# Convolution weights, conditioning columns and the copied sums outside the stages' pools, discarded products in PSUM, one unit moved, in a two-layer transformer step

## The chip, the cores and the metric

One NeuronCore of a Trainium2 chip runs one program. The metric is device microseconds of that core for one execution; a version's time is the median of its runs. Engines in the text: TensorE (PE), VectorE (DVE), ScalarE (ACT), GpSimd (POOL) and SyncE (SP, which here only issues DMAs).

## The reference

Two sequences of 128 tokens (a prompt and a sample with cached context of 128 more) pass through two layers with 2048 features, in fp32. Each layer has six modulation vectors of 2048 entries per sequence: shift, scale and gate for the mixer (j = 0, 1, 2) and for the feed-forward part (j = 3, 4, 5). Layer 0's mixer joins latent attention and grouped-query attention, layer 1's is differential attention. All weights come from memory once.

```
mod = silu(cond) @ w_ada[l] + b_ada[l]          # 2048 -> 6 * 2048, for each sequence
h = rmsnorm(x, g_norm_mix[l]) * (1 + sc1) + sh1
x = x + gt1 * mixer(h)
h = rmsnorm(x, g_norm_ffn[l]) * (1 + sc2) + sh2
u = h @ w_up                                    # 2048 -> 2 * 5632
u = u[t-1] * w_conv[0] + u[t] * w_conv[1] + u[t+1] * w_conv[2] + b_conv
x = x + gt2 * ((silu(gate) * val) @ w_down)     # gate, val: the halves of u
```

## The kernel before

Both sequences are kept side by side: a tile of activations has 128 features on the partitions and 2 x 128 tokens along it. A product (`gemm`, L226) takes blocks of 128x128 weights; each weight and each activation is split in a high and a low part (`split`, L186: ACT casts, DVE subtracts), and three matmuls per block (L233 to L235) add up in one PSUM tile, `acc`, of which there are three. A weight tile of 1 MB (`raw`, three buffers) is loaded by SyncE (L208) and split into `wh` and `wl` of 8 blocks each, four buffers of each (L215, L216). An up product has 16 blocks (48 matmuls), a down product 22 (66).

The program runs in stages: `ab` (layer 0's mixer: input projection, heads, output projection), `ffn0`, `c` (layer 1's mixer), `ffn1`. Each stage opens its own pool of SBUF tiles, which lies over the memory of the pools closed before it; what is needed throughout lies in the pool `keep`. All eight PSUM banks are given out once: `pacc` 3, `pada` 1, `patt` 3, `pmisc` 1 (L83 to L86).

**The modulation vectors** are made beside the rest. One unit (l, j, q) is a quarter of one vector, 512 entries, from 4 MB of `w_ada` in four loads. There are three ways:

- A unit in the list `ROWS` is normally summed on PE (`sum_rows`, L318): the weights move, the conditioning columns (`condw`, 32 columns per block) stand (L322), into the bank `ada`. ACT copies the sums to SBUF as `am` (L263), PE transposes them (L269), and DVE adds them up and adds the bias `bada` (L278, L280).
- If its index is in `SUMMED`, DVE multiplies and adds the weights (L348, L351) into `aacc`, and PE only sums over the partitions (L256, four matmuls) before the copy and two transposes.
- A unit in the list `FEATS` is made of eight feature steps (L306): DVE multiplies 2048 weights by a row of the conditioning (`condb`) and adds up on the way. The products themselves are thrown away: they are written to `junk`, a bf16 tile in the FFN's pool. L313 adds the bias.

`pump(rows, feats)` (L372) is called after every product and issues as many of these steps as have come due by the stage's rate: `RATE` for rows, `FRATE` for feature steps (0.68 per up product, 1.47 per down product; none in the first three pairs of up products and in the last four down products). `RLIMIT` and `FLIMIT` say up to which unit a stage may go. `fill(units)` issues whole units at once, at the start of `ffn0`, `c` and `ffn1`, while the norm is made and modulated (`modulated`, L433). A scheduler then orders the instructions of each engine by a simulated timeline; calls in `keep_in_program_order` stay in their order.

**Who owns which tile.** `condw` is built by `set_condw` (L117) at the start of `ab` in the pool `rows` and again at the start of `c` in the pool `cc`: POOL clears it, ACT fills two of 32 columns. `am` and `aacc` lie in the same pools. The convolution's weights `convw` (176 KB) lie in the FFN's pool and are loaded at its start (L851, L854). The convolution itself (`conv`, L857) reads `acc`: ACT multiplies and adds the bias (L859), DVE adds the two neighbours (L862, L865). At the start of `ffn` and of `c` a list of tiles is made in advance (L850 to L853, L925 to L928), which lays the pool out in that order.

**Order at an FFN's start.** `modulated` issues `ensure`, the norm, the modulation of 16 chunks and `fill`; then `ffn` loads `convw`, and products run with their convolutions. `load_row` (L292) loads `condb` (2 MB) and applies silu after the first product.

Of the kernel before, what the change touches and what calls it, by code (L numbers as in the profile page):

```python
# [17 lines left out]
P = 128  # L18
# [19 lines left out]
    ("cond", 32), ("bada", NL * 6 * 32),  # L38
    ("gmix", NL * 32), ("gffn", NL * 32), ("gfin", 16),
# [9 lines left out]
RATE = {"in": 0.4, "in3": 0.25, "heads": 0.85, "out0": 1.2, "c": 0.75, "outc": 0.75}  # L49
FRATE = {"up": 0.68, "down": 1.47}  # L50
# [10 lines left out]
ROWS += [(1, 2, 1), (1, 2, 2), (1, 2, 3)]  # L61
# [13 lines left out]
def step_kernel(ctx: ExitStack, tc: tile.TileContext, A: dict):  # L75
# [41 lines left out]
    def set_condw(pl):  # L117
        ada["condw"] = T_(pl, [P, KD, 32], "condw")
        pool.memset(ada["condw"], 0.0)
        act.activation(ada["condw"][:, :, 0:2], C("cond").rearrange("p (k r) -> p k r", r=2), AF.Silu)  # L120
# [34 lines left out]
    def rstd(ps, n):  # L155

        v = T_(small, [P, 16], "rv")
        dve.tensor_scalar(out=v[:, :n], in0=ps, scalar1=EPS, scalar2=None, op0=ALU.add)
        r = T_(small, [P, 16], "rr")
        pool.tensor_tensor(out=r[:, :n], in0=v[:, :n], in1=C("mhalf")[:, :n], op=ALU.pow)  # L160
        return r
# [84 lines left out]

    def ada_finish(l, j, q, on_dve):
# [3 lines left out]
        def reduce():  # L251
            ps = T_(pada, [P, 512], "ada")
# [13 lines left out]
        def turn():  # L266
            pt = T_(pada, [P, 512], "ada")
# [3 lines left out]
            bias = C("bada").rearrange("p (l j k r) -> p l j k r", l=NL, j=6, k=KD)[:, l, j, 4 * q:4 * q + 4]  # L271
# [13 lines left out]
    def scales(l, j, q, out):  # L285
        if j in (1, 4):
            g_ = C("gmix" if j == 1 else "gffn").rearrange("p (l k r) -> p l k r", l=NL, k=KD)
            dve.scalar_tensor_tensor(out=scl[:, l, j // 4, 4 * q:4 * q + 4], in0=out, scalar=1.0,
                                     in1=g_[:, l, 4 * q:4 * q + 4], op0=ALU.add, op1=ALU.mult)
# [8 lines left out]
    def feature_step():  # L298
# [4 lines left out]
        if c == 0:  # L303
# [3 lines left out]
            out=T_(feat["pool"], [P, D], "junk", mybir.dt.bfloat16), in1=feat["row"][:, c],  # L307
# [765 lines left out]
```

## Time and profile before

| | |
|---|---|
| runs before | 2515.49, 2517.92, 2518.29 us; median 2517.92 us |
| profiled execution | 2521.01 us, span 2518.9 us, granted clock 0.983 |
| instructions | 47341 |
| DMA | 613 MB, 243 GB/s over the span |
| stages in the span (about) | `ab` to 484 us, `ffn0` to 1268 us, `c` to 1716 us, `ffn1` to 2507 us |

A page of the profile gives each engine's busy time, then 40 slices of the span with the busy share in tenths, then the chain of work that ended last, then groups of instructions. `L233 PE MATMUL acc<-hx,wh` is the instruction of line 233, which reads `hx` and `wh` and writes `acc`; `x4208 | 1199.8, 286 | 22.1` are its count, its busy time in us, the mean of one in ns, and the idle time of the engine just before these instructions. A view of waits says `PE acc L233 <- DVE cv L865: 14.6, 2, 8.2`: matmuls of line 233 waited 14.6 us in all for line 865 on DVE, two times, at most 8.2 us. A timeline gives start and length in us, and in brackets how long the engine had been idle and what released it. Matmul records overlap: one lasts 0.28 us, but in a stretch without a gap the next starts 0.12 us later.

### The profile page before, as it was taken

How to read it: one execution, taken by the hardware profiler on the slowest of the kernel's cores; microseconds unless marked ns; L12 is line 12 of the kernel's file. 1: busy time of each engine (PE TensorE's matmuls, PEld its weight loads, DVE VectorE, ACT ScalarE, POOL GpSimd, SP SyncE). 2: the span in 40 equal slices, each digit the busy share in tenths (PEclk: the TensorE clock that was granted, in tenths of full speed). 3: DMA queues.
4: the chain of work that ended last, by engine and by line, in shares of the span. 5: the costliest groups of instructions: out<-in, count | busy, mean ns of one | idle time of the engine just before them, and what ended most of it. 6: DMA issues, size and time to landing. Idle time of an engine off the chain costs nothing.

```text
span 2518.9 us, 47341 instructions
## 1 busy us (share of the span) xinstructions
PE 2440.5 (97%) x19674; PEld 2300.5 (91%) x19674; DVE 1775.3 (70%) x2715; ACT 1155.7 (46%) x1817; POOL 173.0 (7%) x212
## 2 busy tenths in 40 slices
PE   6999999989999999999999999998999999999997
PEld 3778868789999999999979999896999999999997
DVE  2457534558888888889869897885787645666644
ACT  3335543454443344544455454435544433555442
POOL 2002101200000000001210100021000000000011
PEclk8999999999999999999999999998999999999999
DMA  9886667766667776667776777677565555555553
GB/s 378 311 306 239 246 247 296 292 251 250 250 232 262 282 268 247 234 252 266 268 278 236 277 247 280 224 300 303 201 251 185 184 182 181 182 182 181 183 183 117
DMA packets 92549, 613.05 MB, mean 243 GB/s; under 512 B 9968, under 2 KB 17840, under 8 KB 20400
## 3 DMA queue, kind: packets, MB, share of 16 engines
q1 hardware_dynamic: 92336, 610.04, 66.5%
q8 instruction: 154, 2.52, 0.4%
q14 instruction: 59, 0.48, 0.1%
HBM read 605.25 MB, written 4.75 MB: 242 GB/s over the span
## 4 chain that ended last, share of the span: by engine, by line
PE 95%; DMA 2%; DVE 1%; issue 1%; ACT 1%; POOL 0%; POOLq 0%; SPq 0%; DVEq 0%; ACTq 0%
PE acc L233 29%; PE acc L234 29%; PE acc L235 29%; PE ada L322 4%; DMA araw<-w_ada 1%; PE att L493 1%; DMA raw<-w_ada 1%; PE ada L269 1%; DMA raw<-w_in_ab 0%; DMA convw<-wconv 0%; PE att L782 0%; PE att L483 0%; PE ada L256 0%; DVE x L941 0%; ACT wh L187 0%
## 5 line engine op out<-in xcount | busy, mean ns | idle before, releaser
L187 ACT CAST wh<-raw 128x1024 fp32r<-128x1024 f32 (+1 forms) x788 | 790.4, 1008 | 1136.9 <-PE acc L234 955.8
L188 DVE TENSOR_TENSOR wl<-raw,wh 128x1024 fp32r<-128x1024 f32 (+1 forms) x788 | 925.6, 1182 | 493.7 <-ACT wh L187 479.5
L233 PE MATMUL acc<-hx,wh 128*128 128x256 f32 x4208 | 1199.8, 286 | 22.1 <-DVE cv L865 14.6
L234 PE MATMUL acc<-hx,wh 128*128 128x256 f32 x4208 | 1198.3, 285 | 0.0
L235 PE MATMUL acc<-hx,wl 128*128 128x256 f32 x4208 | 1196.5, 285 | 0.0
L233 PEld LDWEIGHTS acc<-hx,wh 128*128 128x128 f32 x4208 | 810.3, 193 | 52.8 <-ACT cv L859 14.9
L234 PEld LDWEIGHTS acc<-hx,wh 128*128 128x128 f32 x4208 | 811.3, 193 | 23.6 <-issue 20.0
L235 PEld LDWEIGHTS acc<-hx,wl 128*128 128x128 f32 x4208 | 811.2, 193 | 12.2 <-issue 12.1
L234 PE MATMUL acc<-g,wh 128*128 128x256 f32 x1408 | 398.2, 283 | 0.0
L235 PE MATMUL acc<-g,wl 128*128 128x256 f32 x1408 | 398.0, 283 | 0.0
L233 PE MATMUL acc<-g,wh 128*128 128x256 f32 x1408 | 397.8, 283 | 0.0
L234 PEld LDWEIGHTS acc<-g,wh 128*128 128x128 f32 x1408 | 270.3, 192 | 0.0
L235 PEld LDWEIGHTS acc<-g,wl 128*128 128x128 f32 x1408 | 270.2, 192 | 0.0
L233 PEld LDWEIGHTS acc<-g,wh 128*128 128x128 f32 x1408 | 270.1, 192 | 0.0
L306 DVE CUSTOM_DVE_ANT_0 junk<-araw,condb 128x2048 bf16<-128x2048 f32 x112 | 255.5, 2281 | 0.0
L153 POOL TENSOR_TENSOR sqacc<-sqacc,sq 128x256 f32<-128x256 f32 x76 | 94.2, 1240 | 1650.3 <-issue 1319.7
L322 PE MATMUL ada<-araw,condw 128*32 128x512 f32 x864 | 122.1, 645 | 22.2 <-DMA araw<-w_ada 20.1
L351 DVE SCALAR_TENSOR_TENSOR aacc<-araw,condw,aacc 128x512 f32<-128x512 f32 x180 | 132.7, 763 | 0.3
L859 ACT ACTIVATE cv<-acc,convw 128x256 f32<-128x256 f32 x176 | 98.2, 560 | 10.2 <-DMA convw<-wconv 10.2
L444 DVE SCALAR_TENSOR_TENSOR x<-acc,mod,x 128x128 f32<-128x128 f32 x192 | 58.1, 344 | 61.4 <-PE acc L235 61.4
L862 DVE SCALAR_TENSOR_TENSOR cv<-acc,convw,cv 128x254 f32<-128x254 f32 x176 | 83.6, 475 | 9.0 <-ACT cv L859 9.0
L865 DVE SCALAR_TENSOR_TENSOR cv<-acc,convw,cv 128x254 f32<-128x254 f32 x176 | 84.2, 480 | 3.9
(195 smaller groups left out, 1617.7 us busy)
## 6 DMA issues: line engine op xcount, KB each, us to landing
araw<-w_ada SPq DMA_DIRECT2D x188, 1024.0 KB, 5.7
raw<-w_up SPq DMA_DIRECT2D x176, 1024.0 KB, 4.9
raw<-w_down SPq DMA_DIRECT2D x88, 1024.0 KB, 4.9
raw<-w_in_c SPq DMA_DIRECT2D x48, 1024.0 KB, 5.0
raw<-w_in_ab SPq DMA_DIRECT2D x20, 1024.0 KB, 7.4
raw<-w_out_ab SPq DMA_DIRECT2D x16, 1024.0 KB, 6.4
raw<-w_out_c SPq DMA_DIRECT2D x16, 1024.0 KB, 5.9
raw<-w_q_up SPq DMA_DIRECT2D x6, 768.0 KB, 4.5
```

Of the source, the lines that this page charges most:

```text
L153: pool.tensor_tensor(out=st["acc"], in0=st["acc"], in1=sq, op=ALU.add)
L187: act.copy(out_hi, src)
L188: dve.tensor_tensor(out=out_lo, in0=src, in1=out_hi.bitcast(F32), op=ALU.subtract)
L233: pe.matmul(ps[:, :n], wh, xh(k), start=(i == 0), stop=False)
L234: pe.matmul(ps[:, :n], wh, xl(k), start=False, stop=False)
L235: pe.matmul(ps[:, :n], wl, xh(k), start=False, stop=(i == last))
L306: tc.keep_in_program_order(dve.tensor_tensor_reduce(out=T_(feat["pool"], [P, D], "junk", mybir.dt.bfloat16), in1=feat["row"][:, c], in0=fe ...
L322: i = pe.matmul(ada["ps"][32 * g:32 * g + 32, :], ada["condw"][:, 4 * t + g, :], raw[:, g], start=(t == 0), stop=(t == 3), skip_group_chec ...
L351: i = dve.scalar_tensor_tensor(out=acc[:, c], in0=raw[:, g], scalar=ada["condw"][:, k, c:c + 1], in1=acc[:, c], op0=ALU.mult, op1=ALU.add)
L859: act.activation(y, ps, AF.Identity, scale=cw[:, 1, m:m + 1], bias=cw[:, 3, m:m + 1])
L862: dve.scalar_tensor_tensor(out=y3[:, :, 1:], in0=p3[:, :, :T - 1], scalar=cw[:, 0, m:m + 1], in1=y3[:, :, 1:], op0=ALU.mult, op1=ALU.add)
L865: dve.scalar_tensor_tensor(out=y3[:, :, :T - 1], in0=p3[:, :, 1:], scalar=cw[:, 2, m:m + 1], in1=y3[:, :, :T - 1], op0=ALU.mult, op1=ALU.add)
```

## The change

- `condw`, `convw` stand in `keep`, `am` in `tmp`. `condw` is built once. `convw` is loaded by `load_cw(0)` ahead of the heads of layer 0, and by `load_cw(1)` after the modulation at the start of stage `c`, into the one buffer.
- The pool `rows` and the lists of tiles made in advance are gone.
- The PSUM banks of `pada` and `patt` are allotted by stage: in `ab` and in `c` a pool holds `ada` (1) and `att` (3); in each FFN a pool of four banks holds `junk`, now [128, 2048] in fp32.
- Unit (1, 2, 1) moves from `ROWS` to `FEATS`, so that the units of `ROWS` behind it move up by one: `fill` at the start of `c` takes (1, 2, 2) and (1, 2, 3) instead of (1, 2, 1) and (1, 2, 2), and the first unit that the pump makes in `c`, index 23, is (1, 4, 0) instead of (1, 2, 3). `SUMMED` has five indices instead of six, all in `c`. Stage `c` has 8 units of the pump instead of 9, three of them on PE in both. FFN 0 has 13 feature units instead of 12 (104 steps instead of 96); FFN 1 has two in both.
- `RATE` and `FRATE` are changed to go with that.
- `bada`, `gmix` and `gffn` are stored once for both sequences and read with a repeated element; the table of constants has 1397 columns instead of 1653.
- `rstd`'s small tiles have 2 columns instead of 16.

The diff, cut to its core:

```diff
-    ("cond", 32), ("bada", NL * 6 * 32),
-    ("gmix", NL * 32), ("gffn", NL * 32), ("gfin", 16),
+    ("cond", 32), ("bada", NL * 6 * KD),
+    ("gmix", NL * KD), ("gffn", NL * KD), ("gfin", 16),
...
-RATE = {"in": 0.4, "in3": 0.25, "heads": 0.85, "out0": 1.2, "c": 0.75, "outc": 0.75}
-FRATE = {"up": 0.68, "down": 1.47}
+RATE = {"in": 0.4, "in3": 0.25, "heads": 0.85, "out0": 1.2, "c": 0.65, "outc": 0.65}
+FRATE = {"up": 0.75, "down": 1.55}
...
-ROWS += [(1, 2, 1), (1, 2, 2), (1, 2, 3)]
+ROWS += [(1, 2, 2), (1, 2, 3)]
...
-FEATS += [(1, 2, 0)]
+FEATS += [(1, 2, 0), (1, 2, 1)]
...
-RLIMIT = {"ab": 20, "ffn0": 21, "c": 32, "ffn1": 34}
-FLIMIT = {"ab": 0, "ffn0": 12, "c": 12, "ffn1": 14}
-SUMMED = [23, 25, 26, 28, 29, 31]
+RLIMIT = {"ab": 20, "ffn0": 21, "c": 31, "ffn1": 33}
+FLIMIT = {"ab": 0, "ffn0": 13, "c": 13, "ffn1": 15}
+SUMMED = [23, 25, 26, 28, 30]
...
-    pada = ctx.enter_context(tc.tile_pool(name="pada", bufs=1, space=PSUM))
-    patt = ctx.enter_context(tc.tile_pool(name="patt", bufs=3, space=PSUM))
     pmisc = ctx.enter_context(tc.tile_pool(name="pmisc", bufs=1, space=PSUM))
+    ppool = {}
+
+    def banks(name):
+        return tc.tile_pool(name=name, bufs=1, space=PSUM)
...
-    def set_condw(pl):
-        ada["condw"] = T_(pl, [P, KD, 32], "condw")
-        pool.memset(ada["condw"], 0.0)
-        act.activation(ada["condw"][:, :, 0:2], C("cond").rearrange("p (k r) -> p k r", r=2), AF.Silu)
+    condw = T_(keep, [P, KD, 32], "condw")
+    pool.memset(condw, 0.0)
+    act.activation(condw[:, :, 0:2], C("cond").rearrange("p (k r) -> p k r", r=2), AF.Silu)
+
+    def load_cw(l):
+        ada["cw"] = T_(keep, [P, 4, 2 * NFF], "convw")
+        sp.dma_start(out=ada["cw"], in_=A["wconv"][:, l])
...
-            ps = T_(pada, [P, 512], "ada")
+            ps = T_(ppool["ada"], [P, 512], "ada", bufs=1)
...
-            am = T_(ada["pool"], [P, 512], "am", bufs=1)
+            am = T_(tmp, [P, 512], "am", bufs=1)
...
-        feat["row"] = T_(feat["pool"], [P, 2, D], "condb")
+        feat["row"] = T_(feat["home"], [P, 2, D], "condb")
...
-            out=T_(feat["pool"], [P, D], "junk", mybir.dt.bfloat16), in1=feat["row"][:, c],
+            out=T_(feat["pool"], [P, D], "junk"), in1=feat["row"][:, c],
...
-        pt = T_(patt, [P, 512], "att")
+        pt = T_(ppool["att"], [P, 512], "att", bufs=3)
...
                 o = T_(keep, [P, KD, 2 * NT], "hx", F32R)
+                load_cw(0)
...
-        with tc.tile_pool(name=f"ffn{l}", bufs=1) as fp:
-            T_(fp, [P, 2 * NT], "g", F32R, bufs=KQ)
-            cw = T_(fp, [P, 4, 2 * NFF], "convw")
-            T_(fp, [P, NT], "cv", bufs=3)
-            T_(fp, [P, D], "junk", mybir.dt.bfloat16)
-            sp.dma_start(out=cw, in_=A["wconv"][:, l])
-            feat["pool"] = fp
+        cw = ada["cw"]
+        with tc.tile_pool(name=f"ffn{l}", bufs=1) as fp, banks(f"pffn{l}") as pf:
+            feat["home"], feat["pool"] = fp, pf
...
-    with tc.tile_pool(name="rows", bufs=1) as rows:
-        ada["pool"] = rows
-        set_condw(rows)
+    with banks("pab") as ppool["ada"]:
+        ppool["att"] = ppool["ada"]
...
-    with tc.tile_pool(name="cc", bufs=1) as cp:
-        T_(cp, [P, KD, 2 * NT], "oall", F32R, bufs=1)
-        for tag, w, bufs in (("dq", 512, 2), ("dk", 768, 2), ("dv", 768, 2), ("dev", 256, 2),
-                             ("p0", 384, 1), ("p1", 384, 1), ("pT", 384, 2), ("on", 512, 1)):
-            T_(cp, [P, w], tag, bufs=bufs)
+    with tc.tile_pool(name="cc", bufs=1) as cp, banks("pc") as ppool["ada"]:
         ada["pool"] = cp
-        set_condw(cp)
+        ppool["att"] = ppool["ada"]
         hx = modulated(st, 1, 0, 2)
+        load_cw(1)
```

More of the change, by code (lines that the diff above doesn't have):

```diff
@@ L245, in step_kernel, with vector @@
     later = []
+    def vector(name, l, j, q):
+        at = (l * _AT[name][1] // NL) + j * KD + 4 * q
+        return C(name)[:, at:at + 4, None].to_broadcast([P, 4, 2])
     def ada_finish(l, j, q, on_dve):
@@ L266, in turn @@
         def turn():
-            pt = T_(pada, [P, 512], "ada")
+            pt = T_(ppool["ada"], [P, 512], "ada", bufs=1)
             for b in range(2 if on_dve else 4):
@@ L270, in turn @@
             out = mod[:, l, j, 4 * q:4 * q + 4]
-            bias = C("bada").rearrange("p (l j k r) -> p l j k r", l=NL, j=6, k=KD)[:, l, j, 4 * q:4 * q + 4]
+            bias = vector("bada", l, j, q)
             if on_dve:
@@ L311, in feature_step @@
         if feat["t"] == 8:
-            bias = C("bada").rearrange("p (l j k r) -> p l j k r", l=NL, j=6, k=KD)[:, l, j, 4 * q:4 * q + 4]
-            dve.tensor_tensor(out=out, in0=out, in1=bias, op=ALU.add)
+            dve.tensor_tensor(out=out, in0=out, in1=vector("bada", l, j, q), op=ALU.add)
             scales(l, j, q, out)
@@ L319, in sum_rows @@
         if t == 0:
-            ada["ps"] = T_(pada, [P, 512], "ada")
+            ada["ps"] = T_(ppool["ada"], [P, 512], "ada", bufs=1)
         for g in range(4):
-            i = pe.matmul(ada["ps"][32 * g:32 * g + 32, :], ada["condw"][:, 4 * t + g, :], raw[:, g],
+            i = pe.matmul(ada["ps"][32 * g:32 * g + 32, :], condw[:, 4 * t + g, :], raw[:, g],
                           start=(t == 0), stop=(t == 3), skip_group_check=True)
@@ L347, in row_step @@
                 if k == 0:
-                    i = dve.tensor_scalar(out=acc[:, c], in0=raw[:, g], scalar1=ada["condw"][:, k, c:c + 1],
+                    i = dve.tensor_scalar(out=acc[:, c], in0=raw[:, g], scalar1=condw[:, k, c:c + 1],
                                           scalar2=None, op0=ALU.mult)
@@ L351, in row_step @@
                     i = dve.scalar_tensor_tensor(out=acc[:, c], in0=raw[:, g],
-                                                 scalar=ada["condw"][:, k, c:c + 1], in1=acc[:, c],
+                                                 scalar=condw[:, k, c:c + 1], in1=acc[:, c],
                                                  op0=ALU.mult, op1=ALU.add)
@@ L992, in _layout @@
     f["cond"] = np.stack([_feat(i["c_ctx"]), _feat(i["c"][0])], -1)
[L993 to L996 removed]
+    f["bada"] = _feat(i["b_ada"])
+    f["gmix"] = _feat(i["g_norm_mix"])
+    f["gffn"] = _feat(i["g_norm_ffn"])
     f["gfin"] = _feat(i["g_final"])
```

28 lines of the change are left out of this document (12 added, 16 removed).

## The prediction

> **What bounds the kernel now.** I read the page first (busy shares, slices), then TensorE's waits, then the timeline at the places that the waits name, then windows for the stretches between.
>
> ```profile
> PE 2440.5 (97%) x19674; PEld 2300.5 (91%) x19674; DVE 1775.3 (70%) x2715; ACT 1155.7 (46%) x1817; POOL 173.0 (7%) x212
> ...
> PE   6999999989999999999999999998999999999997
> ...
> DVE  2457534558888888889869897885787645666644
> ```
> ```profile
> PE ada L322 <- DMA araw<-w_ada: 20.1, 7, 7.9
> PE acc L233 <- DVE cv L865: 14.6, 2, 8.2
> ```
>
> TensorE (PE) is busy 97% of the span of 2518.9 us. What it loses, it loses in few places: the start, and the stage borders (slices 8, 28 and the last). The second largest wait, 14.6 us in two pieces, is a matmul that needs an accumulator which the convolution has not yet emptied. Those are the two starts of the FFN stages:
>
> ```profile
> 516.82 0.28 PE L235 MATMUL acc<-hx,wl 128*128 128x256 f32 x1
> 523.45 0.55 PE L233 MATMUL acc<-hx,wh 128*128 128x256 f32 x1 [6.36 <-DVE cv L865]
> ```
> ```profile
> 506.91 1.05 ACT L187 CAST wh<-raw 128x1024 fp32r<-128x1024 f32 x1 [2.01 <-PE acc L234]
> 508.47 1.05 ACT L187 CAST wh<-raw 128x1024 fp32r<-128x1024 f32 x1 [0.51 <-PE acc L234]
> ...
> 521.38 1.48 ACT L859 ACTIVATE cv<-acc,convw 128x256 f32<-128x256 f32 x3 [3.32 <-DMA convw<-wconv]
> ```
> ```profile
> 516.47 0.33 SPq L854 DMA_DIRECT2D convw<-wconv  x1
> ```
> ```profile
> 1750.61 0.66 PE L269 MATMUL ada<-cst,am 128*128 128x128 f32 x4 [0.71 <-ACT am L263]
> 1759.46 0.55 PE L233 MATMUL acc<-hx,wh 128*128 128x256 f32 x1 [8.20 <-DVE cv L865]
> ```
> ```profile
> 1751.35 0.33 SPq L854 DMA_DIRECT2D convw<-wconv  x1
> ```
>
> The load of the convolution weights (convw) is issued only at 516.47 and 1751.35, each time just behind the last transposes of a conditioning unit (L269): its tile lies in the stage's pool, over the memory of the copied sums (am). By then three products fill all three accumulators, and the convolutions (L859) wait for the landing. In between, the FFN stage has no gap at all:
>
> ```profile
> 557.00:800.00 243.00, 243.00 (x2028) 243.00 (x2027) 212.92 (x269) 116.92 (x158) 0.00 (x0) 1.00 0.68 247
> 800.00:925.00 125.00, 125.00 (x1044) 125.00 (x1043) 110.35 (x131) 49.43 (x54) 0.00 (x0) 1.00 0.76 278
> 925.00:1140.00 215.00, 215.00 (x1794) 215.00 (x1793) 188.19 (x243) 107.42 (x150) 0.00 (x0) 1.00 0.67 241
> 1140.00:1241.00 101.00, 101.00 (x844) 101.00 (x844) 94.21 (x105) 42.03 (x53) 19.26 (x11) 1.00 0.76 275
> sum 684.00, PE 684.00 PEld 684.00 DVE 605.67 ACT 315.81 POOL 19.26; mean PE 171.00 PEld 171.00 DVE 151.42 ACT 78.95 POOL 4.82
> ```
>
> These are up, down, up, down of layer 0 (columns: length, busy PE, PEld, DVE, ACT, POOL, clock, DMA share, GB/s). PE is full; VectorE (DVE) has 684.0 - 605.7 = 78 us to spare, but only 6.8 of the 101 us of the last one.
>
> **The change part by part.**
>
> *Convolution weights outside the stage.* The loads go out during the heads of layer 0 and at the start of stage c. They then stand behind nothing of the FFN's start: convw has its own place, am and the columns (condw) too, so the FFN's pool lies only over tiles long read. What is late next? The cast at 508.47 got its buffer from the product before the last, so the first two products were done by 508.5, and their convolutions can run some 8 us before the third ends at 516.9. ACT and DVE have room there; the fourth product's weights are cast from 506.9 on. I see nothing that holds PE, and take both waits whole: 6.4 + 8.2 = **14.6 us**. The 0.71 us at L269 goes too if matmuls of the fourth product can stand ahead of it; between 0 and 0.7 I take 0.7, since they then have what they need.
>
> After each wait PE also restarts at half clock:
>
> ```profile
> 523.45:527.00 3.55, 3.55 (x17) 3.55 (x17) 1.88 (x5) 2.55 (x5) 0.00 (x0) 0.50 0.95 402
> 527.00:530.55 3.55, 3.55 (x31) 3.55 (x31) 0.00 (x0) 3.55 (x3) 0.00 (x0) 1.00 0.18 74
> ...
> 1759.46:1763.00 3.54, 3.54 (x18) 3.54 (x19) 1.87 (x5) 3.11 (x5) 0.00 (x0) 0.56 0.84 356
> 1763.00:1766.55 3.55, 3.55 (x33) 3.55 (x32) 0.00 (x0) 3.55 (x3) 0.00 (x0) 1.00 0.02 9
> ```
>
> 17 and 18 matmuls where the next equal window does 31 and 33: 14 and 15 lost, at 3.55/31 = 0.115 us and 3.55/33 = 0.108 us; 1.6 + 1.6 us. Single records lack in these counts, so I take **3.0 us** for both. The two issues themselves (0.33 us of SyncE's queue, 176 KB) move into stretches with spare DMA; only the one at stage c can stand ahead of a load that PE waits for (below). I charge 0.3 us.
>
> *Columns outside the stage.* First the span in which the feature steps run in FFN 0, then TensorE at the start of stage c:
>
> ```profile
> L306 DVE CUSTOM_DVE_ANT_0 junk<-araw,condb x96: 2275/2281/2289, 557.1 to 1238.3; 128x2048 bf16<-128x2048 f32 x96
> ```
>
> ```profile
> 1268.11 0.28 PE L167 MATMUL misc<-cst,sqacc 128*128 128x1 f32 x2
> 1269.47 1.92 PE L322 MATMUL ada<-araw,condw 128*32 128x512 f32 x16 [1.08 <-ACT condw L120]
> 1271.32 0.38 PE L168 MATMUL misc<-cst,sq 128*128 128x1 f32 x2
> ...
> 1277.82 1.93 PE L322 MATMUL ada<-araw,condw 128*32 128x512 f32 x8 [3.35 <-DMA araw<-w_ada]
> ```
>
> The 16 matmuls wait 1.08 us for the columns, which are built anew in the new pool, and then stand ahead of L168, the second half of the norm's sums, and of the buffers' release for the next load, which ends the chain at 1277.82. With columns that never go away all of this moves up by that wait: **1.1 us**. The added wait is that these matmuls' bank must be given back by the discarded products; behind it in PE's queue stand L168 and the whole norm. The last feature step starts at 1238.3 and is over 28 us earlier, so I price it at 0; if the last step slid to the stage's end, it would cost what it slid beyond 1268.
>
> *One unit moved* (layer 1, gate 2, quarter 1) from stage c's sums on DVE to feature steps in layer 0's FFN. In c it takes away 30 L351, 2 L348 (off PE's path) and, on PE, two groups of four L256 and two transposes:
>
> ```profile
> 1703.25 0.28 PE L235 MATMUL acc<-oall,wl 128*128 128x256 f32 x1
> 1703.46 0.62 PE L256 MATMUL ada<-aacc,cst 128*32 128x256 f32 x4
> 1704.02 0.38 PE L233 MATMUL acc<-oall,wh 128*128 128x256 f32 x1
> ```
>
> From matmul to matmul 0.77 us where 0.12 is usual: 0.65 per group, twice, and some 0.15 for the transposes: **1.4 us**, in a stage where PE is 99% busy. The four loads move with it, into a stretch with a DMA share of 0.65 to 0.76.
>
> In FFN 0 it adds eight steps:
>
> ```profile
> L306 DVE CUSTOM_DVE_ANT_0 junk<-araw,condb 128x2048 bf16<-128x2048 f32 x112 | 255.5, 2281 | 0.0
> ...
> L306 DVE DVE_READ_ACCUMULATOR2_ANT mod<- 128x1 f32 x112 | 9.1, 82 | 0.0
> ```
>
> 8 x 2.36 = 18.9 us on DVE, PE untouched as long as there is room. The rates split 104 steps as before: up 82 x 0.75 = 61.5 (was 55.8), down 28 x 1.55 = 43.4 (was 41.2). So the up stretches (458 us, DVE idle 56.9) take 13.5 us more and keep 43; the down stretches (226 us, idle 21.4) take 5.3 more and keep 16. The weights are split up to four half products ahead, so PE bears a DVE that is some us late. Their first step waits for the banks that the transposes of L269 leave (read by 517), but comes only at about 557. I price it at 0; if the cover were gone, every us of DVE beyond it is a us of the end.
>
> *Discarded products in PSUM.* No row of before shows DVE writing PSUM. The rows nearest to it, by form, and DVE's split of the weights within FFN 0 (min/median/max):
>
> ```profile
> L862 DVE SCALAR_TENSOR_TENSOR cv<-acc,convw,cv 128x254 f32<-128x254 f32 x176 | 83.6, 475 | 9.0 <-ACT cv L859 9.0
> ...
> L428 ACT CAST hx<-nt 128x256 fp32r<-128x256 f32 x64 | 22.6, 399 | 4.0 <-DVE nt L424 3.8 <-DVE mod L278 0.2
> ...
> L635 ACT COPY proj<-acc 128x256 f32<-128x256 f32 x15 | 5.5, 371 | 5.8 <-PE acc L235 5.8
> ...
> L794 DVE SCALAR_TENSOR_TENSOR p<-p,drec,p 128x256 f32<-128x256 f32 x8 | 3.8, 479 | 0.0
> ```
> ```profile
> L188 DVE TENSOR_TENSOR wl<-raw,wh x267: 677/1224/1759, 531.5 to 1266.4; 128x1024 fp32r<-128x1024 f32 x124, 128x512 fp32r<-128x512 f32 x10
> ```
>
> From below: ACT's copy out of PSUM (371 ns) is 28 ns under its cast within SBUF (399 ns); a step may win as little. From above: the slowest split took 1759 ns where the median is 1224, x1.44; for this step 3.28 us. The nearest row is DVE's own: with one operand in PSUM (acc, L862) it took 475 ns, with all in SBUF (L794) 479; and PE writes PSUM at 0.12 us per 256 columns, 0.47 ns each, while this step delivers one element per 1.1 ns. I take 2281 ns unchanged, 0 us.
>
> The Trainium skill (Perfetto Trace Analysis, Optimizing Scalar/DVE Operations) puts DVE's access overhead per instruction at about 60 ns on SBUF and 125 ns on PSUM. By it 104 steps would need some 7 us more of DVE (an estimate), the down stretches would keep about 13 us, and the third rival below would be nearer, though the sum stays. For reads the trace does not bear it out (475 against 479 ns above); for writes no run here shows it.
>
> *Constants stored once per column.* The table shrinks by 256 of 1653 columns, 128 KB:
>
> ```profile
> 0.00:40.00 40.00, 17.47 (x90) 4.24 (x90) 6.85 (x19) 13.05 (x28) 11.95 (x20) 0.82 0.97 391
> ```
>
> With DMA 97% busy at 391 GB/s up to 40 us, 128 KB are **0.3 us**. Reading a bias with a repeated element instead of a stored pair touches 128x8 operations only: 0.
>
> Sum: 14.6 + 0.7 + 3.0 - 0.3 + 1.1 + 1.4 + 0.3 = 20.8 us. The profiled execution took 2521.0 us (span 2518.9 and 2.1 around it), so it would become 2500.2; it lies 3.1 us above the median of the runs, 2517.9, so the median becomes **2497**.
>
> **The rivals.**
> *Another wait takes its place (2503).* If the convolution's own tile (cv) still had to wait for the release at 516.47 and 1751.35, only the landing would go: 521.38 - 516.47 = 4.9 us, and at the second start about the same or 1 us more. That is 10 to 11 us, perhaps half of the clock's 3.0, and the small terms (1.1 + 1.4 + 0.3 - 0.3): some 15. For it: the load waited at exactly that point. Against: what lay there (am, condw) is moved out.
> *The change doesn't do what it says (2515).* The load for a layer is queued behind something as late as now, or new bank waits eat what they give: only the small terms stay, 2.8 us. Against it, SyncE loads for stage c 20 us before FFN 0 ends, so an early load is indeed early:
>
> ```profile
> 1247.17 17.96 SPq L208 DMA_DIRECT2D raw<-w_in_c  x4
> ```
> *DVE crowds PE in the down stretches (2503, 6 us lost).* The 16 us left there are an average, and a DVE late by more than the weights' lead stalls PE; a step 0.5 us longer gives the same, 43.4 x 0.5 - 16.3 = 5.4 us. For it: 6.8 us idle in the last 101. Against: not one PE wait in 527 to 1268 now.
> *Slower: the PSUM write is slow, DVE sets FFN 0's pace (2542).* At 3.28 us per step 104 steps add 104 us; the room is 59: 45 us on the end, none in FFN 1 with 16 steps. It begins at +0.38 us per step (down) and outweighs the gain from +0.77 us, 3.05 us per step. Against: the rows above.
>
> **How the numbers follow.** Forecast 0.66 (2492 to 2502); another wait 0.12; DVE crowded 0.08; no effect 0.07; slower 0.07. A measurement of this kernel tells about 0.2%, 5 us, from no change: faster 0.86, same 0.07, slower 0.07. The range 2489 to 2510 holds the first three, and leaves out the last two. Its low end grants 8 us more, of which I can name only the 3.35 us wait at 1277.82; the rest is for an order of instructions that comes out otherwise. Its high end is a step 0.65 us longer: 43.4 x 0.65 - 16.3 = 12 us.
>
> **What would show it.** Right: no wait L233 <- DVE cv; convw landed before 500 and before 1740; no half-clock window at the FFN starts; L306 near 2281 ns; PE full from the start of FFN 0 to its end; 40 L256 instead of 48. Wrong: L306 over 2.66 us with PE waiting for wl in down; L859 waiting for anything but PE at an FFN start; L322 at the start of c waiting for DVE.

## The result, and the profile after

The kernel after takes 2488.47 us (median of 4 runs, 2483.7 to 2491.76) where the kernel before took 2518.11 beside it (4 runs): a ratio of 0.9882, 95% interval 0.9864 to 0.9901. It is 29.6 us faster. The prediction said 20.8 us faster, 2497.0 us, with a range down to 2489. The profiled execution after took 2491.76 us, with a span of 2489.7.

First the waits of PE after (us in total, times, longest), where before had 14.6 us for `cv`:

```profile
PE ada L333 <- DMA araw<-w_ada: 19.6, 7, 7.4
PE acc L240 <- ACT hx L439: 9.5, 6, 2.9
...
PE att L835 <- DVE on L828: 3.4, 1, 3.4
...
PE acc L240 <- ACT cv L867: 0.2, 1, 0.2
```

The wait for the convolution is gone but for 0.2 us. The loads of its weights and the first three convolutions of FFN 0 after show how:

```profile
L127 SPq DMA_DIRECT2D convw<-wconv x2: 328/328/328, 14.9 to 1128.3; - x2
...
DMA to landing us min/median/max: 4.5/7.1/9.7
```
```profile
509.84 0.56 ACT L867 ACTIVATE cv<-acc,convw 128x256 f32<-128x256 f32 x1
510.30 1.04 ACT L194 CAST wh<-raw 128x1024 fp32r<-128x1024 f32 x1
511.24 0.56 ACT L867 ACTIVATE cv<-acc,convw 128x256 f32<-128x256 f32 x1
511.70 1.04 ACT L194 CAST wh<-raw 128x1024 fp32r<-128x1024 f32 x1
512.63 0.57 ACT L867 ACTIVATE cv<-acc,convw 128x256 f32<-128x256 f32 x1
```

The loads are issued at 14.9 and 1128.3 us, hundreds of us before their use, and ACT runs the convolutions between its casts. So far the prediction. But the gain is larger than the waits, and the rest of it stands where nobody waits for anything. These are equal windows in the second `up` of FFN 0, before and then after (length, then busy us and count for PE, PEld, DVE, ACT, POOL; clock; DMA share; GB/s):

```profile
900.00:1080.00 180.00, 180.00 (x1502) 180.00 (x1502) 158.49 (x203) 90.23 (x127) 0.00 (x0) 1.00 0.68 248
```
```profile
900.00:1080.00 180.00, 180.00 (x1519) 180.00 (x1518) 164.03 (x210) 90.92 (x127) 0.00 (x0) 1.00 0.70 258
...
780.00:840.00 60.00, 60.00 (x502) 60.00 (x502) 56.09 (x63) 21.65 (x22) 0.00 (x0) 1.00 0.76 290
```

PE is busy throughout at a granted clock of 1.00 in all three, yet after fits 1519 matmuls into the 180 us that held 1502 (one or two at the edges are counted whole). The last row is a `down` stretch of after, whose matmuls read `g`: 502 in 60 us, 120 ns each as before. The busy share does not show this gain, since it is 100% either way; a count in a window does. From here on "spacing" is the time from the start of one matmul to the start of the next, taken from the records, without those over 160 ns. Before, it is 120.00 ns for both `hx` and `g` in the FFNs, and 119.7 to 119.9 for `hx` in the mixers. After, it is 118.6 to 118.7 ns for `hx` in every stage, and still 120.0 for `g`.

Stage by stage, in the two profiled executions (us; the spread of the norm is the matmul L182 of before, L189 of after, that hands the norm's factor to all partitions):

| stretch | before | after | change | of it from the spacing of `hx` |
|---|---|---|---|---|
| start to the spread of the norm for FFN 0 | 486.4 | 483.7 | -2.7 | -1.9 |
| from there to the end of `up` 1, FFN 0 | 275.00 | 263.81 | -11.2 | -2.75 |
| `up` 2, each FFN | 253.60 | 250.79 | -2.8, twice | -2.8, twice |
| `down`, four of them | 126.9 | 126.9 | 0.0 | 0 |
| FFN 0 to the first matmul on `hx` in `c` | 11.41 | 10.69 | -0.7 | 0 |
| `c`, to its last matmul on `oall` | 436.71 | 437.60 | +0.9 | -2.5 |
| spread of the norm for FFN 1 to the end of `up` 1 | 276.46 | 266.65 | -9.8 | -2.76 |

The last column adds up to 15.5 us less (in each stretch the time between matmuls on `hx`, after less before), about half of the 29.2 us between the two spans, and no step of the prediction has it. What the waits and all else gave is 13.7 us.

### The profile page after: what moved, and what is told of

It reads as the page before. It is cut to its first block, busy times and chain, and to the rows that moved or that the text cites. A ratio compares the mean times of both kernels' runs of the same rounds, so it can differ in the third digit from the quotient of the medians.

```text
span 2489.7 us, 47301 instructions
## 1 busy us (share of the span) xinstructions
PE 2424.8 (97%) x19664; PEld 2284.3 (92%) x19664; DVE 1767.7 (71%) x2699; ACT 1155.9 (46%) x1815; POOL 167.2 (7%) x211
## 4 chain that ended last, share of the span: by engine, by line
PE 94%; DMA 2%; issue 1%; DVE 1%; ACT 1%; POOL 0%; POOLq 0%; SPq 0%; DVEq 0%; ACTq 0%
PE acc L240 29%; PE acc L241 29%; PE acc L242 29%; PE ada L333 4%; DMA araw<-w_ada 1%; PE att L504 1%; DMA ckc<-cache_ckv 1%; PE ada L281 1%; DMA raw<-w_in_ab 0%; PE att L794 0%; PE att L494 0%; DMA raw<-w_ada 0%; DVE x L945 0%; PE ada L268 0%; DVE nt L435 0%
## 5 line engine op out<-in xcount | busy, mean ns | idle before, releaser
L240 PEld LDWEIGHTS acc<-hx,wh 128*128 128x128 f32 x4208 | 793.7, 189 | 47.5 <-ACT hx L439 19.7
L241 PEld LDWEIGHTS acc<-hx,wh 128*128 128x128 f32 x4208 | 795.0, 189 | 21.0 <-issue 19.4
L242 PEld LDWEIGHTS acc<-hx,wl 128*128 128x128 f32 x4208 | 795.2, 189 | 12.2 <-issue 12.1
L318 DVE CUSTOM_DVE_ANT_0 junk<-araw,condb 128x2048 f32<-128x2048 f32 x120 | 274.8, 2290 | 0.0
L160 POOL TENSOR_TENSOR sqacc<-sqacc,sq 128x256 f32<-128x256 f32 x76 | 88.0, 1158 | 1613.1 <-issue 1282.1
L362 DVE SCALAR_TENSOR_TENSOR aacc<-araw,condw,aacc 128x512 f32<-128x512 f32 x150 | 107.8, 748 | 0.3
```

Source lines behind the costliest of these rows:

```text
L160: pool.tensor_tensor(out=st["acc"], in0=st["acc"], in1=sq, op=ALU.add)
L240: pe.matmul(ps[:, :n], wh, xh(k), start=(i == 0), stop=False)
L241: pe.matmul(ps[:, :n], wh, xl(k), start=False, stop=False)
L242: pe.matmul(ps[:, :n], wl, xh(k), start=False, stop=(i == last))
L318: tc.keep_in_program_order(dve.tensor_tensor_reduce(out=T_(feat["pool"], [P, D], "junk"), in1=feat["row"][:, c], in0=feat["raw"].rearrange ...
L362: i = dve.scalar_tensor_tensor(out=acc[:, c], in0=raw[:, g], scalar=condw[:, k, c:c + 1], in1=acc[:, c], op0=ALU.mult, op1=ALU.add)
```

## The experiments

**Where the faster spacing comes from.** The matmuls are the same instructions with the same data. What differs is where the program places their operands. The pool `keep` now holds `condw` and `convw` and a smaller table, so `hx` and, by another amount, the weight tiles behind it have moved. In bytes of a partition, worked out from the order and sizes of the tiles in the program:

```
          hx      wh (first)   from wh to hx    over 256
before    42592   116320       -73728           0
after     43616   118752       -75136           128
```

All weight tiles and the buffers `raw` that they are made from lie at whole multiples of 512 B from one another; so "distance to wh" stands for the distance to any of these. The pools `tmp` and `small` move together with them, and no run parts those from the weights. The high and the low half of a chunk of `hx`, `g` or `oall` are 1024 B each.

*The kernel before, with the distance of after.*

```diff
         hx = T_(keep, [P, KD, 2 * NT], "hx", F32R)
+        T_(keep, [P, 96], "gap")
...
-        v = T_(small, [P, 16], "rv")
+        v = T_(small, [P, 2], "rv")
```

> The kernel before, with 384 B left empty in each partition between hx and the weight tiles, so that the distance from hx to wh is 74112 B, which leaves 384 over whole 512s, as in the kernel after (75136), where before had 73728 (0 over). The rv and rr tiles are 2 columns wide instead of 16, to make the room. Nothing else differs. Theory 1 (the place of hx against the weight tiles sets the pitch of the matmuls): matmuls that read hx start 118.7 ns apart instead of 120.0 in the up stages and instead of 119.8 in the mixers, 12,432 of them, so 15 to 16 us less: 2502 to 2503 us; matmuls that read g stay at 120.0. Theory 2 (the faster pitch comes from something else that the change did: less writing into SBUF by the feature step, the banks of PSUM, the shape of the table): pitch 120.0, 2517 to 2519 us. Theory 3 (it differs from build to build or from run to run): the pitch is anything, and not the same in all of this call's kernels of one layout.

(hx has 12,624 matmuls, three lines of 4208; the 12,432 here and below is a slip that changes 0.3 us.) Measured: 2505.49 us against 2517.86, ratio 0.995 (0.9937 to 0.9962), 12.4 us less. The window of the `up` stretch in it:

```profile
900.00:1080.00 180.00, 180.00 (x1519) 180.00 (x1519) 158.31 (x206) 91.11 (x128) 0.00 (x0) 1.00 0.68 248
```

1519, as after. Spacing of `hx` 118.65 to 118.8 ns in all stages, of `g` 119.99. With next to none of the change (only the two small tiles) a gap of 384 B makes some 40% of its gain. The median gain is less than the 15 to 16 expected, but its interval is 9.6 to 15.9 us, and the two profiled spans differ by 15.2 (2518.9 and 2503.7). `c` is only 1.2 us shorter (435.54) where its spacing gives 2.4; what takes the rest back there, no run shows.

*The kernel after, with the distance of before.*

```diff
         hx = T_(keep, [P, KD, 2 * NT], "hx", F32R)
+        T_(keep, [P, 32], "gap")
```

> The kernel after, with 128 B left empty between convw and the weight tiles, so that the distance from hx to wh is 75264 B, a whole number of 512s as in before. Nothing else differs. Theory 1 (place): the pitch of matmuls that read hx goes back to 120.0 in the up stages, and the kernel takes 2503 to 2505 us; what is then left of the gain on before, 13 to 15 us, is that of the waits. Theory 2 (something else that the change did): 118.7 ns and 2487 to 2490 us, as the kernel after.

Measured: 2505.70 us, ratio 0.995 (0.9936 to 0.9963), and 1503 matmuls in the window:

```profile
900.00:1080.00 180.00, 180.00 (x1503) 180.00 (x1502) 163.26 (x208) 89.98 (x126) 0.00 (x0) 1.00 0.70 253
```

So 128 B cost 17 us here (2488.47 to 2505.70; 12.4 us the other way round in the kernel before), and the change itself, without the luck of the place, is worth 12.2 us (9.3 to 16.1). Theory 2 is out, and so is theory 3 at these two distances; at 64 B something like it comes back below.

*The kernel after, all places moved, the distances kept* (64 B ahead of `x`).

```diff
+    T_(keep, [P, 16], "front")
     x = T_(keep, [P, KD, NT], "x")
```

> The kernel after with 64 B left empty ahead of x: x, hx, convw, the weight tiles, g and oall all move by 64 B together, so that every distance between them is that of after and every place is another. Theory 1 (the distance between the moving tile and the weights decides): hx at 118.7 ns, g at 120.0, oall at 120.0, 2486 to 2491 us. Rival (the place of one of them alone decides, over 128 or 256 B): another pitch for hx or g, and 5 to 40 us of difference.

Measured: 2487.83 us, ratio 0.988 (0.9866 to 0.9893); `hx` 118.67, `g` 119.99, `oall` 120.00 ns. With every place moved by 64 B and the distances kept, nothing changes: it is the distance, not a place.

*Other distances for `g` and `oall`.*

```diff
             feat["home"], feat["pool"] = fp, pf
+            T_(fp, [P, (32, 16)[l]], "gap")
...
         ada["pool"] = cp
+        T_(cp, [P, 8], "gap")
```

> The kernel after, with 128 B left empty ahead of g in the first FFN, 64 B in the second and 32 B ahead of oall, so that the distances to wh leave over 512: 128 for g in the first FFN and for oall, 64 for g in the second, where after has 0, 96 and 0; hx stays at 384 over. Theory 1 (distance from the moving tile to the weights, the same in steps of 256 B): in the first FFN's down stages the pitch falls from 120.0 to about 118.7 ns, 2112 matmuls, 2.8 us; oall's 768 matmuls to about 118.7 as well, 1.0 us; the 64 of the second FFN is a place not seen yet, between a gain of 2.8 us and a loss as large: 2482 to 2488 us in all. A theory of the weight tiles' place alone, or of hx's alone: g stays at 120.0 and the time at 2487 to 2490.

Measured: 2482.21 us, ratio 0.9857 (0.9844 to 0.9871). Two windows in `down` stretches, of FFN 0 (128 B) and FFN 1 (64 B), 502 and 252 in after:

```profile
780.00:840.00 60.00, 60.00 (x508) 60.00 (x508) 56.38 (x65) 22.10 (x21) 0.00 (x0) 1.00 0.79 289
...
2000.00:2030.00 30.00, 30.00 (x257) 30.00 (x256) 15.18 (x19) 10.96 (x11) 0.00 (x0) 1.00 0.55 199
```

`g` follows the distance too: 118.66 ns at 128, as `hx` and `oall` (118.62) there; at 64 it is 117.78.

**What the parts of the change are worth.** *Convolution weights alone, in the kernel before, the distance kept.*

```diff
-            cw = T_(fp, [P, 4, 2 * NFF], "convw")
+            cw = ada["cw"]
-            sp.dma_start(out=cw, in_=A["wconv"][:, l])
...
                 o = T_(keep, [P, KD, 2 * NT], "hx", F32R)
+                load_cw(0)
...
         hx = modulated(st, 1, 0, 2)
+        load_cw(1)
...
+        T_(keep, [P, 32], "gap")
         rb0 = norm_scale(st)
```

> The kernel before with one part of the change: the convolution weights in a tile of the outer pool, loaded ahead of the stage as in the kernel after, and 128 B left empty behind it, so that hx and the weight tiles stand at 75264 B, a whole number of 512s as in before. Theory A (as predicted: the two waits for the convolution weights go, and the half clock behind them): 6.4 + 8.2 + some 3.0 us less, 2499 to 2502 us, and no wait of the matmuls for cv. Theory B (the moved loads are only a part, and the wait behind them is that for condw or for the sums' copy): the first FFN gives 7 to 9 us, the second only 2 to 5, so 2505 to 2510 us.

Measured: 2503.90 us, ratio 0.9945 (0.9932 to 0.9957): 14.0 us, between the two theories in the median. The stages speak for A in size: spread of the norm to the end of `up` 1 takes 267.1 us in FFN 0 and 268.2 in FFN 1, so 7.9 and 8.3 us less, where B gave the second 2 to 5. But A had no wait for `cv`, and one stays in FFN 1, right behind the transposes of a unit, as B had it in kind:

```profile
PE acc L237 <- DVE cv L869: 2.2, 1, 2.2
```

*Banks by stage and the products in PSUM alone, in the kernel before.*

```diff
-            out=T_(feat["pool"], [P, D], "junk", mybir.dt.bfloat16), in1=feat["row"][:, c],
+            out=T_(feat["psum"], [P, D], "junk"), in1=feat["row"][:, c],
...
-        with tc.tile_pool(name=f"ffn{l}", bufs=1) as fp:
+        with tc.tile_pool(name=f"ffn{l}", bufs=1) as fp, banks(f"pffn{l}") as feat["psum"]:
```

> The kernel before with one part of the change: the banks of PSUM allotted by stage, and the discarded products of the feature step as full floats in PSUM (the pools in SBUF are as before but for the empty place of the discarded tile; all distances to the weights as before). As predicted (the step stays near 2281 ns and nothing on the path changes): 2515 to 2520 us. Rival (the release of the banks at a stage's border holds the first matmuls or features): 2 to 6 us slower, to be seen between the last matmul on g and the first on hx of the next stage.

Measured: 2517.10 us, ratio 0.9997 (0.9988 to 1.0006): nothing. The step itself (ns min/median/max):

```profile
L308 DVE CUSTOM_DVE_ANT_0 junk<-araw,condb x112: 2282/2290/2296, 556.2 to 1911.6; 128x2048 f32<-128x2048 f32 x112
```

9 ns more than in bf16 into SBUF (2281). The rival's wait at the borders does not come: from the last matmul on `g` to the first on `hx` of `c` it is 10.1 us, before 11.4.

*`condw` and `am` back in the stages' pools, in the kernel after.*

```diff
-            am = T_(tmp, [P, 512], "am", bufs=1)
+            am = T_(ada["pool"], [P, 512], "am", bufs=1)
...
+        set_condw(cp)
         hx = modulated(st, 1, 0, 2)
```

> The kernel after with condw and the sums' copy (am) back in the stages' pools, where before had them; convw stays outside. The distances of hx and g to the weights are those of after, oall's is 0 over 512 (120.0 ns there too). As predicted (1.1 us of wait for condw at the start of c, 0.7 for the copy at the second FFN): 1.5 to 2 us slower, 2489 to 2491, with the wait of ada for condw of about 1 us back in the list. Rival (the wait stands beside others that end later: nothing is gained): 2487 to 2489, the start of c within 0.3 us of after's.

Measured: 2492.59 us, ratio 0.9903 (0.9889 to 0.9918), against after's 0.9882 (0.9864 to 0.9901): the intervals overlap, and the two spans differ by 0.8 us (2490.5 and 2489.7). The wait for `condw` is back, and yet the start of `c` is 9.2 us long where after's is 10.7. TensorE there, with `condw` in the stage's pool, and then after:

```profile
1253.70 1.93 PE L334 MATMUL ada<-araw,condw 128*32 128x512 f32 x16 [1.09 <-ACT condw L124]
...
1259.83 1.93 PE L334 MATMUL ada<-araw,condw 128*32 128x512 f32 x8 [1.13 <-DMA araw<-w_ada]
```
```profile
1251.56 1.92 PE L333 MATMUL ada<-araw,condw 128*32 128x512 f32 x16
...
1260.33 1.94 PE L333 MATMUL ada<-araw,condw 128*32 128x512 f32 x8 [3.26 <-DMA araw<-w_ada]
```

After saves 1.09 us at the first row and waits 2.1 us more for a load at the second. That load sets when `c` begins; it comes 1.1 to 3.4 us late in these runs, which is more than the term. So nothing is shown for it, either way.

At the start of FFN 1 a wait for `cv` is back as well, although `convw` has long landed. The convolutions on ACT (L868), which let the accumulators be freed, come only behind the last transposes of a unit (L282), which read `am`. The second row is that of FFN 0, where PE has no wait from it; in FFN 1 three convolutions run in one go from 1733.00 us, behind transposes of 1731.85:

```profile
PE acc L241 <- DVE cv L874: 3.5, 1, 3.5
```
```profile
512.63 1.02 ACT L868 ACTIVATE cv<-acc,convw 128x256 f32<-128x256 f32 x2 [1.71 <-PE ada L282]
```

With the 2.2 us in the run with `convw` alone, this is the second kernel in which `am` and `condw` stand in the stage's pool and a wait for `cv` remains; in after it is gone. This is, in small, the prediction's rival of the next wait (`cv`'s own tile waits for the release). So moving the loads ends the wait in FFN 0, and in FFN 1 it takes the move of `am` and `condw` too. Yet the stretch to the end of `up` 1 is only 0.5 us longer than after's (267.15 and 266.65), because after has other waits there (below).

*The unit moved back, in the kernel after.*

```diff
-ROWS += [(1, 2, 2), (1, 2, 3)]
+ROWS += [(1, 2, 1), (1, 2, 2), (1, 2, 3)]
-FEATS += [(1, 2, 0), (1, 2, 1)]
+FEATS += [(1, 2, 0)]
-SUMMED = [23, 25, 26, 28, 30]
+SUMMED = [23, 25, 26, 28, 29, 31]
...
```

> The kernel after without the moved unit: the lists of units, the sums' list, the limits and the rates of before. Places unchanged. As predicted (the move takes two groups of L256 and their transposes out of stage c, 1.4 us): from the first matmul on hx in c to the end of those on oall 439.0 us where after has 437.6, and 2489 to 2491 in all. Rival (the move with its rates costs the c stage 2 to 3 us: the c stage is 1.9 us longer in the after layout at before's distances than in before, where it should be shorter): 434 to 436 us for that stretch and 2485 to 2488 in all.

Measured: 2486.86 us, ratio 0.9886 (0.9869 to 0.9902); no difference can be told in the whole. The stretch of `c` is 436.65 us, where after has 437.60 and the run with 64 B ahead of `x`, the same program of other places, 438.25: with the move it is 1.0 to 1.6 us longer there, where the prediction had a gain of 1.4, but it misses the rival's 434 to 436. Two such runs alike differ by 0.7 us, so the size is rough. What differs in every trace is the wait for `on` (L828): it is 3.4 us or more in all eight kernels with the moved unit and 1.0 in all six without it. In this run:

```profile
PE att L835 <- DVE on L828: 1.0, 1, 1.0
```

DVE in after, ahead of that step:

```profile
1610.14 4.06 DVE L362 SCALAR_TENSOR_TENSOR aacc<-araw,condw,aacc 128x512 f32<-128x512 f32 x6
1614.44 0.87 DVE L828 SCALAR_TENSOR_TENSOR on<-att,var,cst 128x256 f32<-128x256 f32 x2 [0.25 <-POOL var L825]
1615.24 2.07 DVE L362 SCALAR_TENSOR_TENSOR aacc<-araw,condw,aacc 128x512 f32<-128x512 f32 x3
```

With one unit fewer, the sums of the last unit (L362) fall into the last head, and six of them, 4.06 us, stand ahead of the step that PE waits for. After also waits 1.4 us for `oall`; on the other side, a wait of 1.6 us for `aacc` that this run and before have is gone.

**How far the distance goes.** Two sweeps of the kernel after. The first:

```diff
+        T_(keep, [P, 16], "gap")
...
+            T_(fp, [P, (8, 24)[l]], "gap")
...
+        T_(cp, [P, 16], "gap")
```

> The kernel after with other distances, all else equal: counted from wh, over whole 512s, hx stands at 64 (after: 128), g at 32 in the first FFN and at 96 in the second (after: 0), oall at 160 (after: 96). Seen so far: 0 gives 120.0 ns between matmuls, 256 too, 128 gives 118.7, 64 gave 117.8 for g, 96 gave 120.0 for oall with a mixed pattern. Theory 1 (the distance alone decides, whichever tile it is): hx at 117.8, 12,432 matmuls, 11 us less than after; g at 96 stays at 120.0; g at 32 and oall at 160 are places not seen: 0 to 5 us. 2472 to 2479 us. Rival (each tile has its own best place, and 64 was good for g alone): hx anywhere from 118.7 to 120.0, 2487 to 2505 us.

Measured: 2460.84 us (2448.06 to 2472.89), ratio 0.9778 (0.974 to 0.9816), below both ranges. The second:

```diff
+        T_(keep, [P, 48], "gap")
...
+            T_(fp, [P, (40, 56)[l]], "gap")
...
+        T_(cp, [P, 56], "gap")
```

> The kernel after with other distances, all else equal: hx at 448 over whole 512s (that is 192 over 256), g at 160 in the first FFN and at 224 in the second, oall at 320 (64 over 256). Theory 1a (distance over 256, and the same on both sides of 0): hx as at 64, 117.8 ns, 11 us less than after; g at 160 as at 96, 120.0; g at 224 as at 32 in the run beside it; oall at 117.8, 1.7 us less: 2473 to 2478 us. Theory 1b (not the same on both sides: what counts is which of the two is read ahead of the other): hx at 192 between 117.8 and 121, 2475 to 2515 us.

Measured: 2420.51 us, ratio 0.9622 (0.9607 to 0.9636), outside both ranges. Theory 1a has `hx` at 192 faster, and it is, by more than it said; but 160 is not as 96, nor 224 as 32, so the sides differ, as 1b has it. And the first sweep holds something that no theory had. Its windows in the second `up` of FFN 0 and of FFN 1, and then the second sweep's:

```profile
900.00:1080.00 180.00, 180.00 (x1591) 180.00 (x1590) 170.82 (x218) 95.46 (x132) 0.00 (x0) 1.00 0.74 268
2080.00:2260.00 180.00, 180.00 (x1531) 180.00 (x1530) 118.36 (x160) 91.00 (x128) 0.00 (x0) 1.00 0.54 187
```
```profile
900.00:1080.00 180.00, 180.00 (x1590) 180.00 (x1590) 170.85 (x220) 95.92 (x133) 0.00 (x0) 1.00 0.74 266
2080.00:2260.00 180.00, 180.00 (x1591) 180.00 (x1590) 122.59 (x167) 96.14 (x134) 0.00 (x0) 1.00 0.56 194
```

At 64 B `hx` runs at 113.33 ns in one FFN and at 117.78 in the other, each held over all 2112 matmuls of a stretch; at 192 B it is 113.3 in both. So one distance can have two paces. Both `up` stretches of an FFN keep the same one, and what decides between them is not settled. It fits that the first sweep's four times lie 25 us apart, from 2448 to 2473: the 4224 matmuls of one FFN at the other pace are 18.8 us.

*All three operands at 192, in the kernel after.*

```diff
+        T_(keep, [P, 48], "gap")
...
+            T_(fp, [P, (48, 112)[l]], "gap")
...
+        T_(cp, [P, 24], "gap")
```

> The kernel after with all large operands at the distance that was fastest for hx: counted from wh over whole 256s, hx, g and oall at 192 (over 512: hx 448, g 192 in the first FFN and 448 in the second, oall 192). In the run before, hx at that distance ran at 113.3 ns in both FFNs while g at 160 and 224 took 117.3 and 118.3 and oall at 64 took 117.8. Theory 1 (distance alone, the same for each tile): g at 113.3, 2112 matmuls by 4.0 and 2112 by 5.0 ns, oall 768 by 4.4: 22 us less than that run, 2396 to 2402 us. Rival (192 is good for hx alone, since its pace also hangs on how the tile is stepped through, and g is made of 22 tiles): g at 117 to 120, 2417 to 2425 us.

Measured: 2399.62 us (2398.31 to 2403.69), ratio 0.9535 (0.9522 to 0.9548), 89 us faster than the kernel after. `g` is at 113.33 ns; the `down` stretch holds 531 where after had 502:

```profile
760.00:820.00 60.00, 60.00 (x531) 60.00 (x531) 59.03 (x68) 23.21 (x22) 0.00 (x0) 1.00 0.82 310
```

In `c` the spacing is mixed: 114.6 ns for `hx`, 116.7 for `oall`. There `hx` at the same 192 B has 116.35 ns in the second sweep, so in the mixers the distance alone doesn't set the mean.

*The same distances in the kernel before.*

```diff
+        T_(keep, [P, 16], "gap")
...
+            T_(fp, [P, 48], "gap")
             T_(fp, [P, 2 * NT], "g", F32R, bufs=KQ)
...
+        T_(cp, [P, 48], "gap")
         T_(cp, [P, KD, 2 * NT], "oall", F32R, bufs=1)
```

> The kernel before, with none of the change, and three gaps that set hx, g and oall at 192 over whole 256s from wh. Theory 1 (distance): hx 12,432 matmuls by 6 to 6.6 ns in the FFNs and 2 to 5 in the mixers, g 4224 by 6.6, oall 768 by 6.5: 56 + 8 to 20 + 28 + 5 = 97 to 109 us less, 2409 to 2421 us, with the waits for cv still there. Rival (part of the faster pace in the runs on the kernel after came of what else it changed): less than 70 us.

Measured: 2412.99 us (2412.36 to 2414.89), ratio 0.9587 (0.9573 to 0.96), 104 us less than before, with its wait for `cv` still there:

```profile
PE acc L233 <- DVE cv L866: 14.2, 2, 7.6
```

The change is worth 13.4 us between these two, close to the 12.2 us between before and the kernel after at before's distance. What was measured, by distance from `wh` over whole 256s (`hx` and `g` in the FFNs, `oall` in `c`):

| distance | spacing, ns |
|---|---|
| 0 | 120.0 (`hx`, `g`) |
| 32 | 116.7 (`g`) |
| 64 | 117.8 (`g`, `oall`, `hx`) or 113.3 (`hx`) |
| 96 | 120.0 (`g`, `oall`) |
| 128 | 118.7 (`hx`, `g`, `oall`) |
| 160 | 117.3 (`g`), 118.5 (`oall`) |
| 192 | 113.3 (`hx`, `g`), 116.7 (`oall`, mixed) |
| 224 | 118.3 (`g`) |

The Trainium skill (TensorE: Matmul & The Clock Gate, Step-by-step: what each phase is for) says that loading the next tile's weights takes no read bandwidth of SBUF from the running matmul. With PEld busy for the whole 180 us in each of these windows, the same matmuls take 113.3 to 120.0 ns by the distance between the tile that moves and the weights. The measurement decides: a pace that hangs on this distance does not look like two reads that leave each other alone. Which of the reads waits for which, no run shows. That it is these two reads is argued, not shown, since the other engines write and read `raw`, `wh` and `wl` meanwhile. What speaks against those engines is that the second `up` of FFN 1 in before keeps 120.00 ns with DVE busy 60%, as that of FFN 0 does with 88%:

```profile
2080.00:2260.00 180.00, 180.00 (x1503) 180.00 (x1502) 107.89 (x143) 83.26 (x108) 0.00 (x0) 1.00 0.52 182
```

## Why the prediction was right or wrong, point by point

- **The two waits (14.6).** Right, though the loads went out earlier than foretold (at 14.9 us, not during the heads; the second in FFN 0, not in `c`). Both waits are gone, and the part alone shows 7.9 and 8.3 us in its stages, 14.0 us in its median (10.8 to 17.1), with 2.2 us of wait left in FFN 1. That rest is gone in after, where `am` and `condw` too are out of the stage's pool, as the prediction had argued.
- **The wait at L269 (0.7).** Gone: the waits for `am` are 4.9 us in three pieces where before had 5.7 in four.
- **Half clock behind them (3.0).** Half right. FFN 0's 1.6 us came: `up` 1 gave 11.2 us, of which 6.4 are the wait, 2.75 the spacing and 2.1 are left for it. FFN 1's did not. There the half clock lasts longer at the front, where the matmuls wait for `hx`:

```profile
1707.34 0.80 PE L240 MATMUL acc<-hx,wh 128*128 128x256 f32 x2 [2.49 <-ACT hx L439]
1712.96 0.58 PE L240 MATMUL acc<-hx,wh 128*128 128x256 f32 x1 [0.79 <-ACT hx L439]
```
```profile
1707.34:1710.88 3.54, 3.54 (x16) 2.87 (x20) 1.85 (x5) 3.51 (x4) 0.73 (x1) 0.50 1.00 424
1712.96:1716.50 3.54, 3.54 (x16) 2.87 (x20) 3.43 (x11) 3.42 (x10) 1.91 (x3) 0.50 0.88 331
1720.00:1723.54 3.54, 3.54 (x35) 3.05 (x33) 2.97 (x8) 3.54 (x7) 1.31 (x2) 1.00 0.43 176
```

  What ACT does between the two matmuls is the silu of `condb`. Before issues that load at 1751.7 us, and the kernel with `am` and `condw` put back at 1732.5, each time just behind the last transposes of a unit; after issues it at 1699.8. So the silu, at 1762.24 before, comes between the casts of `hx`:

```profile
1708.91 3.71 ACT L308 ACTIVATE condb<-condb 128x2048 f32<-128x2048 f32 x2
1712.52 0.69 ACT L439 CAST hx<-nt 128x256 fp32r<-128x256 f32 x2
```

  So FFN 1 gave 9.8 us: 8.2 + 0.7 + 2.76 of spacing, less 1.9. That early load is an effect of the change which the prediction did not follow.
- **Columns (1.1) and the issue of the loads (-0.3).** 0.7 us came at the border, near their sum, but a load that comes 1.1 to 3.4 us late sits there; nothing is shown.
- **Constants (0.3).** Not seen: the first matmul on `hx` starts at 40.38 us before and at 40.56 after. The 176 KB of `convw`, issued at 14.9 us, now fall into the same stretch as the 128 KB saved.
- **One unit moved (1.4).** Wrong in sign: `c` is 1.0 to 1.6 us longer with it. The matmuls went as counted:

```profile
L268 PE MATMUL ada<-aacc,cst x40: 379/391/404, 1363.3 to 1632.7; 128*32 128x256 f32 x40
```

  40 instead of 48, but the units behind it came to stand elsewhere in `c`, and that was not looked at.
- **Feature steps on DVE and in PSUM (0).** Right: 2290 ns for 2281, PE full from the start of FFN 0 to its end. The slower rival and the crowded DVE did not occur.
- **The sum.** Wrong in what it left out. The step that failed is the pace of the matmuls: the prediction took it as 0.12 us before and after ("0.12 is usual") and put nothing for it in the sum, and what the edits do to the places of `hx` and the weight tiles was not worked out. The runs showed 120.0 ns before and 118.7 after for `hx`, 15.5 us without a wait. The terms that it did add up to 20.8 us came to 12.2 (median of the kernel after at before's distance), or 13.7 in the profiled executions. Most of what they lack lies in two places: FFN 1's start gave 7.0 us without the spacing where 10.4 were forecast, and `c` is 0.9 us longer (1.9 at before's distance) where 1.4 less were forecast. That the time still came out close to the low end of 2489 us is luck: the shortfall of some 7 us hides half of the spacing's 15.5. The low end granted 8 us, mostly for another order of instructions; what came was another pace, and twice as much.

## What to carry to other kernels

Where an engine is busy 97% of the span, count its instructions in equal windows: the pace inside the busy time can hold more than the waits that one sees (104 us here, against the 14.6 for `cv`). An edit that adds or removes a tile in an outer pool moves everything behind it; work out which operands of the innermost loop change their distance to one another, and measure such an edit once with the old distances restored by a gap, or its own worth can't be read. Then try the distances themselves: three gaps of 64 to 192 B, with no other edit, did three and a half times what this change did.

## What the runs showed of the hardware that was not expected

- The spacing of 128x256 matmuls on split fp32 goes from 113.3 to 120.0 ns (6%) with the distance of the moving tile from the weight tiles over 256 B, at a granted clock of 1.00 and with the same instructions on every engine; 128 B of it are worth 12 to 17 us of 2500.
- One distance (64 B) had two paces in one execution, 113.3 and 117.8 ns, each held through a whole stretch of some 240 to 250 us. Why is open.
- A step of DVE that writes 2048 floats per partition into PSUM takes 2290 ns, into bf16 in SBUF 2281.
- A load whose tile nothing holds is issued at 14.9 us for a use at 510, though in the program it is written behind the input projection, which runs to 225 us.
